# Conditioning by column blocks: shift and scale of the first norm made in four column blocks, with the first pair of row tiles multiplied block by block into held PSUM banks

## The chip, the cores and the metric

The kernel runs on one core of one Trainium2 chip. The metric is the device time of one execution in microseconds; lower is better. The program holds one launch.

## The reference

One layer of a bidirectional encoder is applied to two sequences of 1024 rows and 1024 columns (prompt and sample), each with a conditioning vector c. A final norm follows. Cut to what the change touches:

```python
mod = jax.nn.silu(c) @ w_ada + b_ada
sh1, sc1, ga1, sh2, sc2, ga2 = [m[:, None, :] for m in jnp.split(mod, N_MOD, axis=-1)]
h = rmsnorm(x, g_mix) * (1.0 + sc1) + sh1
z = h @ w_in
q_lat, kv_lat, k_pe, f_in = z[..., :o1], z[..., o1:o2], z[..., o2:o3], z[..., o3:]
y_mla = mla_group(q_lat, kv_lat, k_pe, g_q_lat, w_uq, g_kv_lat, w_ukv)
y_four = fourier_group(f_in, w_four)   # real part of a 2-D FFT, then a small matrix per group
mix = jnp.concatenate([y_mla, y_four], axis=-1) @ w_out
x = x + ga1 * mix
h2 = rmsnorm(x, g_ffn) * (1.0 + sc2) + sh2
ffn = (jax.nn.silu(h2 @ w_gate) * (h2 @ w_up)) @ w_down
return x + ga2 * ffn
```

All is float32. The first two sixths of mod, sh1 and sc1, are the first 2048 columns of w_ada: 8.4 MB that have to be read before any row can be shifted and scaled.

## The kernel before

**Numbers.** A float32 product is made of three matmuls on operands split into a high and a low part (`mm3`, L78 to L80). `split` (L62, L63) makes the parts: a cast on ACT, then a subtraction on DVE that waits for the cast.

**Rows.** The rows of a sequence are reordered so that row tile j and its mirrored tile lie in two tiles u = 0 and 1 of 128 rows. Such a pair k = 0 to 7 (four for each sequence) is the unit of stage 1. For a pair: `x_load` reads the two tiles (0.5 MB each); `norm` squares them on ACT, takes the reciprocal root in six small steps on POOL (`rstd`, L103 to L110) and scales on DVE; `flip` transposes two column groups of 128 at a time on PE and applies scale and shift (s1, sh1) on the way out of PSUM into hf, then splits into hh and hl; `evenodd` adds and subtracts the two halves u on POOL (eo) and splits into eoh and eol; `zproj` multiplies hh and hl by the latent part of the weights (wz, 448 columns, 24 matmuls for each u); `fourier_in` multiplies eoh and eol by the Fourier weights wcs (280 and 256 columns, 24 matmuls each); `latents` transposes the normed latents and stores them.

**Weights.** `prep_wcs` makes a 128-row group of wcs from w_in (loaded as wf) with four matmuls by a small table c2. `wz_split` splits wz. The foldings `fold_q`, `fold_pe` and `fold_out` make products of attention weights and store them for later stages. `extras` is a generator whose pieces lie between the pairs: the rest of `fold_out` and a second pass over w_ada for the gates, 1 MB a chunk.

**Modulation before.** w_ada is read in eight chunks of 128 rows and 2048 columns (`chunk`, 1 MB each). `mod_mm` multiplies each by silu(c), four column groups side by side on 32-wide strips of TensorE, and adds all eight chunks up in one PSUM bank. Only after the eighth can `mod_row` copy the sums out and `mod_vecs` (L146 to L155) transpose them and form s1 and sh1 for all columns; the first `flip` stands behind it.

**Order.** The order on each engine is fixed when the program is built: a scheduler of the framework starts from the order in which the code is written and can move an instruction past others on its engine. At run time each engine takes its list strictly in order and waits on semaphores. Transfers are issued by SP in one list, at most eight in flight; a transfer that waits for an engine holds up all behind it. Tiles with the same tag share memory, so a new tile waits for the last reader of the old one.

**Lines.** w_ada chunk loads L207, their matmuls L216; wf L489, wz L327, x L356; prep_wcs L337 to L347; flip L382 (transposes), L387 and L389 (hf); evenodd L400; zproj's squares L413 and L414, its latents L425 and L426; kv stores L431; latents L440; fold_q L238 and L239; fold_out L251 to L254.

## Time and profile before

| what | value |
|---|---|
| three timed runs | 2041.74, 2043.92, 2044.95 us; median 2043.92 |
| span of the profiled execution (the only time the profile gives for it) | 2043.9 us |
| PE busy in the span | 97% |
| first matmul of the modulation, last chunk's matmul | 11.58 us, 40.80 us |
| s1 and sh1 complete | 45.75 us |
| first product of pair 0 | 48.14 us |
| first product of pair 1 | 81.66 us |
| DMA rate 10 to 20, 20 to 30, 30 to 40 us | 404, 393, 415 GB/s |
| DMA rate 60 to 70 us | 71 GB/s |

The engines are named PE (TensorE matmul), PEld (its weight loads), DVE (VectorE), ACT (ScalarE), POOL (GpSimd) and SP (SyncE, which issues transfers). A row of the timeline has the start, the duration and the operation, the tiles written and read, the shape and the count of instructions merged into it, and in brackets the idle time of the engine just before and what ended it. A float32 matmul that is not split shows as two instructions in the trace, since it takes two passes. The duration of a matmul in a row includes the way through the array; what counts for throughput is the distance from one start to the next.

### The profile page before, as it was taken

Reading aid. Unit: us, or ns where it says so; the run is one execution under the profiler, and the core shown is the slowest. Engines: PE = TensorE matmul, PEld = TensorE weight load, DVE = VectorE, ACT = ScalarE, POOL = GpSimd, SP = SyncE. Lnnn points to the kernel's source line nnn. Section 1 sums busy time; section 2 is a strip of 40 time slices with the busy share of each in tenths; the row PEclk is TensorE's granted clock in tenths of the full one; section 3 lists DMA queues with packets and bytes.
Section 4 is the critical chain, followed back from the end, with each engine's and each line's share of the span. In section 5 each row is a group of like instructions: output and inputs, shape, how many; then the busy total and the mean of one; then the engine's idle time right before and its main releaser. Section 6 shows DMA issues by size and latency. Waiting matters only on the chain.

```text
span 2043.9 us, 27849 instructions
## 1 busy us (share of the span) xinstructions
PE 1986.5 (97%) x9610; PEld 1613.6 (79%) x9610; DVE 1415.6 (69%) x2082; ACT 897.3 (44%) x1741; POOL 832.3 (41%) x1021
## 2 busy tenths in 40 slices
PE   6999999999999999999999999999999999999997
PEld 3788877888787777888888888877788888888876
DVE  3667757766677668878777676777766656667684
ACT  3656635555465554333333365453233333336451
POOL 0555213111313317879779410332654454420142
PEclk8999999999999999999999999999999999999999
DMA  9785694544644375546555587674333232258672
GB/s 363 229 258 180 220 336 132 129 104 106 158 114 129 119 277 192 195 157 210 194 166 196 173 306 251 216 233 140 129 118 103 97 110 103 96 187 276 226 228 89
DMA packets 183817, 370.30 MB, mean 181 GB/s; under 512 B 19004, under 2 KB 60476, under 8 KB 180604
## 3 DMA queue, kind: packets, MB, share of 16 engines
q1 hardware_dynamic: 165004, 310.72, 45.8%
q0 software_dynamic: 18672, 57.81, 9.5%
q8 instruction: 75, 1.23, 0.3%
q14 instruction: 66, 0.54, 0.1%
HBM read 256.46 MB, written 120.39 MB: 184 GB/s over the span
## 4 chain that ended last, share of the span: by engine, by line
PE 52%; DVE 3%; DMA 3%; POOL 1%; issue 1%; ACT 1%; SPq 0%; DVEq 0%; ACTq 0%; POOLq 0%
PE bank L78 17%; PE bank L79 17%; PE bank L80 17%; DVE wl L63 1%; DMA draw<-s_d 1%; ACT wh L62 1%; DMA val<-x_d 1%; DVE val L138 1%; POOL val L138 1%; DMA draw<-t_d 0%; DMA rgu<-in_wgu_dram 0%; DVE val L1610 0%; POOL rs_y L106 0%; DMA draw<-in_w_down_dram 0%; SPq L1570 0%
## 5 line engine op out<-in xcount | busy, mean ns | idle before, releaser
L78 PE MATMUL bank<-H,wh 128*128 128x512 f32 x1224 | 477.8, 390 | 6.9 <-DVE val L138 5.8
L80 PE MATMUL bank<-H,wl 128*128 128x512 f32 x1224 | 476.6, 390 | 0.2 <-DVE wl L63 0.2
L79 PE MATMUL bank<-H,wh 128*128 128x512 f32 x1224 | 476.3, 389 | 0.0
L138 DVE TENSOR_TENSOR val<-bank,val 128x512 f32<-128x512 f32 x244 | 166.7, 688 | 166.9 <-PE bank L80 165.8
L78 PEld LDWEIGHTS bank<-H,wh 128*128 128x128 f32 x1224 | 229.8, 188 | 59.0 <-DVE val L138 8.3
L80 PEld LDWEIGHTS bank<-H,wl 128*128 128x128 f32 x1224 | 229.8, 188 | 50.4 <-DVE wl L63 2.3
L79 PEld LDWEIGHTS bank<-H,wh 128*128 128x128 f32 x1224 | 229.8, 188 | 47.1
L63 DVE TENSOR_TENSOR wl<-draw,wh 128x512 fp32r<-128x512 f32 x286 | 202.2, 740 | 86.3 <-ACT wh L62 85.7
L62 ACT CAST wh<-draw 128x512 fp32r<-128x512 f32 x286 | 169.0, 620 | 158.6 <-PE bank L79 81.6
L79 PE MATMUL bank<-wl,wh 128*128 128x512 f32 x572 | 223.7, 391 | 2.8 <-DVE wl L63 2.8
L138 POOL TENSOR_TENSOR val<-val 128x512 f32<-128x512 f32 x58 | 83.4, 1445 | 343.4 <-DVE val L1584 189.6
L80 PE MATMUL bank<-wh,wl 128*128 128x512 f32 x572 | 222.7, 389 | 0.0
L78 PE MATMUL bank<-wh 128*128 128x512 f32 x572 | 222.6, 389 | 0.0
L62 ACT CAST wh<-rgu 128x512 fp32r<-128x512 f32 x171 | 106.3, 623 | 253.6 <-PE bank L79 192.1
L63 DVE TENSOR_TENSOR wl<-val,wh 128x512 fp32r<-128x512 f32 x133 | 139.7, 1052 | 68.8 <-ACT wh L62 68.7
L63 DVE TENSOR_TENSOR wl<-rgu,wh 128x512 fp32r<-128x512 f32 x171 | 169.1, 989 | 9.7 <-ACT wh L62 9.6
L62 ACT CAST wh<-val 128x512 fp32r<-128x512 f32 x133 | 82.3, 622 | 179.1 <-PE bank L79 156.5
L135 POOL TENSOR_TENSOR val<-rgu 128x512 f32<-128x512 f32 x80 | 114.8, 1435 | 99.2 <-DMA rgu<-in_wgu_dram 95.5
L79 PEld LDWEIGHTS bank<-wl,wh 128*128 128x128 f32 x572 | 107.4, 188 | 28.5 <-DVE wl L63 6.3
L78 PEld LDWEIGHTS bank<-wh 128*128 128x128 f32 x572 | 107.4, 188 | 22.5 <-ACT wh L62 0.2
L80 PEld LDWEIGHTS bank<-wh,wl 128*128 128x128 f32 x572 | 107.4, 188 | 21.9
L135 POOL TENSOR_TENSOR val<-val 128x512 f32<-128x512 f32 x89 | 119.3, 1357 | 1.3
(383 smaller groups left out, 3908.1 us busy)
## 6 DMA issues: line engine op xcount, KB each, us to landing
rgu<-in_wgu_dram SPq DMA_DIRECT2D x86, 512.0 KB
draw<-s_d SPq DMA_DIRECT2D x143, 256.0 KB
s_d<-val POOLq DMA_DIRECT2D x88, 256.0 KB, 3.8
draw<-t_d SPq DMA_DIRECT2D x88, 256.0 KB
s_d<-val SPq DMA_DIRECT2D x66, 256.0 KB
draw<-in_w_down_dram SPq DMA_DIRECT2D x55, 256.0 KB
wada<-in_w_ada_dram SPq DMA_DIRECT2D x13, 1024.0 KB
xt<-in_x_dram SPq DMA_DIRECT2D x16, 512.0 KB
```

The lines of the kernel that those rows point to most:

```text
L62: here["a"] = nc.scalar.copy(hi, src).ins
L63: here["v"] = nc.vector.tensor_tensor(out=lo, in0=src, in1=rd(hi), op=ALU.subtract).ins
L78: nc.tensor.matmul(out, lh, rh, start=first, stop=False, skip_group_check=cont)
L79: nc.tensor.matmul(out, lh, rl, start=False, stop=False, skip_group_check=cont)
L80: nc.tensor.matmul(out, ll, rh, start=False, stop=last, skip_group_check=cont)
L135: return eng.tensor_tensor(out=out, in0=x, in1=y, op=ALU.subtract).ins
L138: return eng.tensor_tensor(out=out, in0=x, in1=y, op=ALU.add).ins
```

## The change

The first 2048 columns of w_ada are laid out anew (wa0) as four blocks. Block b holds, for all 1024 rows, the shift and the scale columns of column groups 2b and 2b + 1. With each block come the raw wf and wz for the same column groups. For each block the kernel multiplies (`block_mm`, 32 matmuls of 128 columns), copies and transposes a short row, forms the two columns of s1 and sh1 for both sequences (`block_vecs`), flips the two groups of pair 0 (`flip(0, b)`), makes their even and odd parts (`evenodd_part`), and adds their part of the four products of pair 0 into four PSUM banks that are held over the loop (`z_mm`, `f_mm`, in `products`, one block late). The evictions become `z_out` and `f_out`. During the loop four banks are left for everything else. fold_q and fold_pe move behind pair 0, with their loads behind the last block; fold_out, the flips of pair 1, the norm of pair 2 and the latents of pair 0 follow in a written order in place of `pair(0)`. The raw wz and two foldings use the tiles of zc and zs of the second sequence, which are made when first needed.

```diff
+        def block_load(b):
+            wt = [w2.tile([P, 4, 512], F32, tag="wada", name="wada", bufs=2) if b % 2 == 0
+                  else w.tile([P, 4, 512], F32, tag=("hh1", "hl1")[i], name="wada1") for i in range(2)]
+            for i in range(2):
+                nc.sync.dma_start(wt[i], a["wa0"][b, i])
+            return wt
+
+        def block_mm(b, wt):
+            pm = bank()[:, :P]
+            for c in range(NC):
+                for j in range(4):
+                    nc.tensor.matmul(pm[32 * j : 32 * j + 32, :], scT[:, c, :], wt[c // 4][:, c % 4, P * j : P * j + P],
+                                     start=(c == 0), stop=(c == NC - 1))
+            mr = stile("modrow")[:, :P]
+            nc.vector.tensor_copy(mr, pm)
+            return mr
...
+        def products(b, u):
+            cs = range(2 * b, 2 * b + 2)
+            z_mm(0, u, pz[u], cs)
+            f_mm(st1["eo", 0][u], u, pc[u], cs)
+
+        for b in range(4):
+            for i in range(2):
+                prep_wcs(2 * b + i, wf[b])
+            wz_split(b, wzr[b])
+            mr = block_mm(b, blk[b])
+            if b > 0:
+                products(b - 1, 0)
+            block_vecs(b, mr)
+            if b > 0:
+                products(b - 1, 1)
+            if b < 2:
+                loads(b + 2)
+            if b == 2:
+                nc.sync.dma_start(ropec, a["ropec"])
+                nc.sync.dma_start(ropes, a["ropes"])
+                x_load(1)
+                fq = fold_loads()
...
+            flip(0, b)
+            evenodd_part(0, b)
+        for u in range(2):
+            z_mm(0, u, pz[u], range(6, 8))
+        norm(1)
+        for u in range(2):
+            z_out(0, u, pz[u])
+        for i in range(2):
+            f_mm(st1["eo", 0, i], i, pc[i], range(6, 8))
+            f_out(0, i, pc[i])
         fold_q(*fq)
-        nc.gpsimd.memset(lw, 0.0)
-        mod_mm(0, 0, ch[0])
-        ch[4] = chunk(4)
...
-        mod_mm(0, 7, ch[7])
-        mod_vecs(mod_row(0), bank, bT, gT, 0, 0, s1, sh1)
-        for g in range(2):
-            flip(0, g)
...
+        fold_pe(wpe, gq)
+        pfirst.close()
+        banks.insert(0, st.enter_context(tc.tile_pool(name="p1_ps", bufs=8, space=PSUM, reuse_waits="tile")))
         nk = len(pairs)
         more = extras()
+
+        x_load(2)
+        next(more)
+        fold_out(0, wo2, wuvT, gq)
+        for g in range(4):
+            flip(1, g)
+        fold_out(1, wo2, wuvT, gq)
+        norm(2)
+        latents(0, 0)
...
-        for k in range(nk - 1):
+        for k in range(1, nk - 1):
             pair(k)
```

How this moves instructions is shown at three places. In the changed file the lines are others: the block matmul is L535, its row's transpose L543, prep_wcs L349, flip L394 with hf at L401, the square of x L378, the squares of the latents L449 and L450, the copies of the Fourier products L505 and L503, x L368, the kv stores L467, the stores of fold_q and fold_pe L254 and L273, the fold_out stores L267, w_out's load L257.

PE before, from the preparation of wcs to the first product; wada and wide are chunks of w_ada in different tiles:

```order
L216 MATMUL bank<-wada,scT 32x512 x4
L337 MATMUL bank<-c_136,wf 128x128 x16
L216 MATMUL bank<-wada,scT 32x512 x4
L216 MATMUL bank<-wide,scT 32x512 x4
L216 MATMUL bank<-wada,scT 32x512 x4
L146 MATMUL bank<-ident,modrow 128x128 x4
L382 MATMUL bank<-ident,xt 128x128 x16
L78 MATMUL bank<-wz_h,hh 128x448
```

PE after, in the loop of blocks, from the preparation of wcs for block 2 to the first half of block 2's matmul (wada, the last row); held is a held bank:

```order
L349 MATMUL bank<-c_130,wf 128x128 x8
L78 MATMUL held<-wz_h,hh 128x448
L79 MATMUL held<-wz_l,hh 128x448
L78 MATMUL held<-wcs_h,eoh 128x280
L79 MATMUL held<-wcs_l,eoh 128x280
L78 MATMUL held<-wz_h,hh 128x448
L79 MATMUL held<-wz_l,hh 128x448
L78 MATMUL held<-wcs_h,eoh 128x256
L80 MATMUL held<-wz_h,hl 128x448
L78 MATMUL held<-wz_h,hh 128x448
L79 MATMUL held<-wz_l,hh 128x448
L535 MATMUL bank<-wada,scT 32x128 x16
```

Before, all flips of pair 0 and all its products stand behind the last chunk's matmul. Now ten products of block 1 stand ahead of the first half of block 2's matmul; thirteen more stand ahead of its second half, and its row's transpose is behind that.

ACT after, from the last block's hf (first row) on; xt in the squares is x of pair 1:

```order
L401 ACTIVATE hf<-bank,sh1b,s1b 128x256
L378 ACTIVATE junk,ms<-xt 128x1024
L62 CAST hh<-hf 128x512
L62 CAST eoh<-eo 128x256 x2
L378 ACTIVATE junk,ms<-xt 128x1024
```

ACT after, a little further, from the Fourier copies of pair 0 to the flips of pair 1; xt in the square is now x of pair 2:

```order
L505 COPY zc_110<-held 128x280
L503 ACTIVATE zs_111<-held,cmask 128x256
L62 CAST kv<-lat 128x128 x2
L378 ACTIVATE junk,ms<-xt 128x1024
L401 ACTIVATE hf<-bank,sh1b,s1b 128x256 x3
L62 CAST hh<-hf 128x512
L401 ACTIVATE hf<-bank,sh1b,s1b 128x256 x2
L62 CAST hh<-hf 128x512
```

ACT before, at the flips of pair 1; the two squares are those of x of pair 2 here too:

```order
L62 CAST kv<-lat 128x128
L413 ACTIVATE junk,mz<-bank 128x256
L414 ACTIVATE junk,mz<-bank 128x128
L366 ACTIVATE junk,ms<-xt 128x1024 x2
L389 ACTIVATE hf<-bank,sh_0_77,s_0_75 128x256
L62 CAST kv<-lat 128x128
L389 ACTIVATE hf<-bank,sh_0_77,s_0_75 128x256 x2
L62 CAST hh<-hf 128x512
```

In both a square of pair 2's x stands ahead of pair 1's hf on ACT. What changed is when that x is asked for. SP before, around the load of pair 2's x (the second row):

```order
L244 DMA wada<-in_w_out_dram 128x2x1024
L356 DMA xt<-in_x_dram 128x1024 x2
L244 DMA wada<-in_w_out_dram 128x2x1024
L260 DMA wq_d<-wq 128x1536
L431 DMA ckv_d_96<-kv 128x128
L431 DMA ckv_d_97<-kv 128x128
```

SP after, around the same load (the sixth row); the two first sequences of kv stores are those of pair 0:

```order
L257 DMA wada<-in_w_out_dram 128x2x1024
L467 DMA ckv_d_94<-kv 128x128
L467 DMA ckv_d_95<-kv 128x128
L467 DMA ckv_d_94<-kv 128x128
L467 DMA ckv_d_95<-kv 128x128
L368 DMA xt<-in_x_dram 128x1024 x2
L254 DMA wq_d<-zraw 256x1x512
L273 DMA wq_d<-wqp 256x1x256
L257 DMA wada<-in_w_out_dram 128x2x1024
```

Before, pair 2's x was asked for ahead of the kv stores of pair 0; now it is asked for behind all four of them.

208 lines of the change are left out of this document (113 added, 95 removed).

## The prediction

> **What bounds the kernel now.** I read the page first, then the busy time by stage, then the order of time on each engine up to 90 us, since only the beginning of the program is rebuilt.
>
> ```profile
> PE 1986.5 (97%) x9610; PEld 1613.6 (79%) x9610; DVE 1415.6 (69%) x2082; ACT 897.3 (44%) x1741; POOL 832.3 (41%) x1021
> PE   6999999999999999999999999999999999999997
> 0.00:20.00 20.00, 10.41 (x48) 4.35 (x48) 2.97 (x10) 1.50 (x2) 1.94 (x9) 1.00 0.83 311
> 20.00:40.00 20.00, 13.55 (x88) 9.76 (x88) 9.62 (x27) 10.10 (x30) 1.74 (x6) 0.82 1.04 404
> 40.00:60.00 20.00, 16.81 (x78) 13.09 (x79) 15.70 (x31) 10.06 (x22) 6.38 (x6) 0.84 0.77 296
> 60.00:81.66 21.66, 17.20 (x88) 12.21 (x86) 14.43 (x29) 12.59 (x30) 13.27 (x31) 0.84 0.56 174
> 81.66:240.00 158.34, 156.15 (x1019) 134.95 (x1018) 108.17 (x237) 94.73 (x242) 75.86 (x168) 1.00 0.69 216
> ```
>
> The columns of a stage are its length, the busy time of PE, PEld, DVE, ACT and POOL (with instructions), the granted clock, the DMA share and GB/s. TensorE (PE) is the bound from 81.66 us on: 156.15 us busy of 158.34. Before that it is busy for 10.41 + 13.55 + 16.81 + 17.20 = 57.97 us of 81.66, so idle for 23.7. From 20 to 40 us the DMA engines are full (404 GB/s), and the modulation weights bound; from 60 to 81.66 they are half idle and a chain through ACT, POOL and DVE bounds. All that the change can win lies in these 23.7 us, and what it wins there arrives at the end of the program, because behind it runs a nearly gapless PE.
>
> ```profile
> 40.80 1.94 PE L216 MATMUL bank<-wada,scT 128*32 128x512 f32 x8 [3.63 <-DMA wada<-in_w_ada_dram]
> 73.25 0.69 PE L78 MATMUL bank<-wcs_h,eoh 128*128 128x280 f32 x1
> 81.66 0.45 PE L78 MATMUL bank<-wz_h,hh 128*128 128x448 f32 x1
> 86.55 1.03 PE L382 MATMUL bank<-ident,xt 128*128 128x128 f32 x8
> ```
>
> The last chunk of w_ada lands at 40.80; the cosine product of the first pair only begins at 73.25; the first product of the second pair runs from 81.66 to 86.55. By 81.66 all of pair 0 and the weight foldings are done, in the changed kernel too, and from there the two kernels' streams hold the same work. So **the gain is 81.66 us less the time at which that product starts after the change**.
>
> **Arrival of the blocks.**
>
> ```profile
> 2.11 0.43 SPq L227 DMA_DIRECT2D wuqT<-in_wuqT_dram  x1
> 5.83 1.62 PE L238 MATMUL bank<-wukT,wuqT 128*128 128x128 f32 x6 [5.83 <-DMA wuqT<-in_wuqT_dram]
> 13.51 0.20 PEld L216 LDWEIGHTS bank<-wada,scT 128*32 128x32 f32 x8 [1.73 <-DMA wada<-in_w_ada_dram]
> ```
>
> By the tile shapes 3.01 MB are in when chunk 1 lands at 13.51, and 13.37 MB when chunk 7 lands at 40.80: 0.38 MB a us. The change asks for 1.05 MB of x and four blocks of 3.08 MB (0.52 of wf, 0.46 of wz, 2.10 of w_ada), 13.37 MB again, with the first large transfer issued behind the small constants at about 3.5 us instead of 1.6. Block 0 is then complete near 17.5 us, a block follows every 8 us, and block 3 is complete between 41 and 42.7, say 41.4: **the loads themselves gain nothing**. A 0.5 MB load takes up to 5.83 - 2.11 = 3.7 us from issue to use.
>
> **The cost of one block.**
>
> ```profile
> 16.00 1.06 PE L216 MATMUL bank<-wide,scT 128*32 128x512 f32 x8 [0.56 <-DMA wide<-in_w_ada_dram]
> 20.07 3.84 PE L337 MATMUL bank<-c,wf 128*128 128x128 f32 x32 [0.44 <-DMA wf<-in_wfT_dram]
> 78.05 0.68 PE L78 MATMUL bank<-wcs_h,eoh 128*128 128x256 f32 x1
> 81.30 0.60 PE L440 MATMUL bank<-ident,lat 128*128 128x128 f32 x4
> ```
>
> The block matmul has 32 matmuls of 32x128, two passes each, 64 in the trace. No row shows that shape. A group of eight 512-wide passes, four column strips abreast, takes 1.06 us, 0.133 each; a quarter of the width gives 0.033, 2.1 us a block and 1.05 for the half behind each transfer. Upwards the bound is a pass of the same width on the full array, 3.84/32 = 0.12, or 7.7 us a block; downwards I exclude a gain, since the same columns stream. I take 0.033, the row of the same line and strips, and keep the other end for a rival. A projection matmul costs 4.89/24 = 0.204 and a Fourier one (81.30 - 78.05)/24 = 0.135, so a block's products (12 of each) are 4.1 us; the preparation of wcs is 16 passes, 1.9 us.
>
> In its third paragraph the section "Wait — 56ns, not 53.3ns?" of the Trainium skill's page "TensorE: Matmul & The Clock Gate" puts a floor of about 25 ns start to start on narrow matmuls, and about 62 ns where matmuls are decoded in software. By 25 ns a block's 64 passes would take 1.6 us, below my 2.1, and nothing changes. By 62 ns they would take 4.0, an estimate that would leave about 2045 us; rival C below is that case, told from rows. The rows here favour the low price: at 16.00 four strips run abreast at 0.133.
>
> ```profile
> 42.80 0.69 DVE L221 COPY modrow<-bank 128x512 f32<-128x512 f32 x1 [1.46 <-PE bank L216]
> 43.64 1.09 PE L146 MATMUL bank<-ident,modrow 128*128 128x128 f32 x4 [0.91 <-DVE modrow L221]
> 45.67 0.56 ACT L389 ACTIVATE hf<-bank,sh,s 128x256 f32<-128x256 f32 x1 [5.61 <-PE bank L382]
> 46.27 0.54 DVE L387 TENSOR_SCALAR hf<-bank,s,sh 128x256 f32<-128x256 f32 x1 [0.52 <-ACT hf L389]
> 47.70 1.30 POOL L400 TENSOR_TENSOR eo<-hf 128x512 f32<-128x512 f32 x1 [19.30 <-DVE hf L387]
> 48.51 1.78 ACT L62 CAST wz_h<-wide 128x896 fp32r<-128x896 f32 x2
> 50.08 2.08 DVE L63 TENSOR_TENSOR wz_l<-wide,wz_h 128x896 fp32r<-128x896 f32 x2
> 50.19 0.62 ACT L62 CAST hh<-hf 128x512 fp32r<-128x512 f32 x1
> 52.08 0.68 DVE L63 TENSOR_TENSOR hl<-hf,hh 128x512 fp32r<-128x512 f32 x1
> 21.67 0.42 DVE L342 TENSOR_TENSOR wcs_l<-bank,wcs_h 128x256 fp32r<-128x256 f32 x1 [9.63 <-ACT wcs_h L341]
> ```
>
> The order shown with the change puts the two halves of block b+1's matmul on PE inside and behind the products of block b, and PE takes them in that order. So the blocks form a loop, whatever has landed. Counted from the end of a block matmul: the row copy (a quarter of 0.69), one transpose and three tiny vector operations end near 1.3 us; hf on ACT (0.56) and then DVE (0.54), one behind the other, end at 2.5. The ACT order has the next block's wz cast (1.78/2 = 0.9) ahead of hh, so hh starts at 2.75 and the first product at 3.4; wz_l (1.04) and hl (0.68) hold DVE until 4.6, or 5.2 where POOL's eo (1.30) runs beside them; eol (two of about 0.42) ends at 5.5 to 6.2. On PE ten products and the first half (1.05) end near 6.8, the rest (2.0) at 8.6, and the second half at 9.2 to 9.8. I take **9.5 us a loop** against 8 us between arrivals: the loop, not DMA, is the new limit. The preparation of the next wcs (1.9) hides in PE's wait between 1.5 and 3.4, its casts behind eol. The four held PSUM banks leave four for all else; in this count each is evicted over 2 us before its next use, so I charge nothing, and where one is not it lengthens the loop by what is missing. So it is with the raw wz and wf in borrowed tiles: their loads wait for splits that end 10 us before the data are due, and 2.1 MB are still in flight then. Block 0's matmul ends at 17.5 + 1.0 = 18.5, block 3's at 18.5 + 3 x 9.5 = **E = 47.0 us**, 5.6 behind its data.
>
> **From E to the second pair.**
>
> ```profile
> 58.37 1.05 ACT L366 ACTIVATE junk<-xt 128x1024 bf16<-128x1024 f32 x1
> 62.32 0.22 POOL L103 TENSOR_SCALAR rs_v<-ms 128x2 f32<-128x2 f32 x1
> 64.54 0.20 POOL L110 TENSOR_TENSOR rs_r<-rs_w,rs_y 128x2 f32<-128x2 f32 x1
> 67.89 0.49 DVE L425 TENSOR_SCALAR lat<-bank,rs_r 128x256 f32<-128x256 f32 x1 [1.38 <-POOL rs_r L110]
> 69.49 0.80 SPq L431 DMA_DIRECT2D ckv_d<-kv  x2
> 72.26 1.49 ACT L389 ACTIVATE hf<-bank,sh,s 128x256 f32<-128x256 f32 x3
> 78.46 0.74 DVE L253 TENSOR_SCALAR so<-bank,gq 128x512 f32<-128x512 f32 x1
> ```
>
> PE is done with pair 0 at about E + 7.5 and then waits. The squares of x (1.05 plus 0.19 of reading out) stand in the order around hh and eoh, the second ends at E + 5.6. POOL then makes three reciprocal roots, 64.74 - 62.32 = 2.4 us each, the last with a slower one: E + 13.0. The latents and the kv split behind it add 1.6. SP issues the load of x 2 only behind the four stores of kv (0.4 each): E + 15.3; it lands 3.7 later, at E + 19.0. ACT's order has the square of x 2 ahead of every hf of pair 1, so **this load is a new wait**: all of pair 1's flips, and DVE's hl and so behind them, stand until it lands. Then ACT needs two squares (2.4), eight hf (1.49/3 = 0.5 each) and four hh (about 0.52), 8.5 us: E + 27.5. The hl of that (0.68) and the eviction (0.74) that frees the product's bank end at E + 28.9 = 75.9. Foldings and flips on PE (8 matmuls in fold_q, 8 of 512 columns, 16 transposes) lie inside these waits; x 1, landing near 45, is covered by the block chain, and the other fold loads by it too. If that cover failed, each would cost its own lateness.
>
> Gain: 81.66 - 75.9 = **5.8 us**. The profile's span is 2043.9 us, the median of the three runs 2043.92, so the same sum holds for both: 2043.9 - 5.8 = 2038.1, **2038 us**. Its own range is 2035 to 2041, from 1 us a loop either way.
>
> **Rivals.**
>
> A. The loop is quicker than the arrivals (its PE and DVE parts overlap better than I stacked them). Then E = 41.4 + 1.0 = 42.4, 4.6 earlier, and the time is **2033.5**. For it: DMA is full in 20 to 40 us. Against: the count of 9.5, in which only about 1 us is generous.
>
> B. It is given back behind E. The second w_ada chunk of the extras is now issued behind the kv stores of pair 1, DVE is by the same count about 5 us behind PE there (xt of x 2, four evictions and four eol stand ahead of the latents), and PE comes out of a wait:
>
> ```profile
> 66.00:70.00 4.00, 4.00 (x12) 2.35 (x11) 2.21 (x8) 1.28 (x4) 3.35 (x11) 0.50 0.02 6
> ```
>
> After such a wait the clock was 0.50 from 66 to 70. A first product at that clock for 3.4 us costs 1.7, a late chunk 2 to 3: about 4 us lost, **2042**, no change that a measurement can tell.
> The section "Part 1: The HAM clock gate (the "warmup" mystery)" of the same page of the Trainium skill says that one idle window of about 3.4 us halves the clock; the row at 66 agrees, and by that rule the new wait would cost an estimated 1.7 us.
>
> C. The narrow strips do not run four abreast at a quarter of the price. At 0.12 a pass the half block costs 3.8, the loop 5.6 more, E 3 x 5.6 + 2.8 = 19.6 more: **2057.7**, slower. It decides from 0.033 + 5.8/224 = 0.059 us a pass (224 passes lie on the path); at 0.062 the time is near 2045. Against it: the strips in the row at 16.00, and no sign of an issue limit there.
>
> That the order does not do what the edit says is excluded by the order itself.
>
> **How the numbers follow.** Forecast 0.50, A 0.20, B 0.20, C 0.10. A measurement of this kernel can tell about 0.2%, 4.1 us. Faster takes A and 0.42 of the forecast's 0.50; same takes the remaining 0.08 and 0.18 of B; slower takes C and 0.02 of B: 0.62, 0.26, 0.12. For the range I leave out the dear end of C and the far end of A: 2032 to 2046.
>
> **What would show it.** The order in time at the start: block matmuls of L535 ending about 9.5 us apart, the last near 47 (A: 8 apart, 42.4; C: 12 or more apart, single passes far above 0.033). ACT's square of x idle before it on the load of x near 62 to 66. The product of pair 1 (L78, bank from hh) starting near 76. From there PE gapless; a gap on w_ada in pair 1, or a clock of 0.50 under its first product, is B. I would be wrong altogether if the PE gaps after that start were not those of before.

## The result and the profile after

The changed kernel takes 2054.07 us, the median of five runs from 2052.87 to 2055.22, against 2043.74 of the kernel before in runs beside it (2039.7 to 2044.95). The ratio is 1.0052, with a 95% interval of 1.0039 to 1.0065: **slower by half a per cent**, where 2038 us was forecast, with a range to 2046. The profiled execution spans 2053.4 us, 9.5 more than before.

The page of the changed kernel (first line) and its busy time by stage, in the same columns as before, cut at the start of pair 1's first product:

```profile
PE 1992.6 (97%) x9802; PEld 1620.0 (79%) x9802; DVE 1407.9 (69%) x2092; ACT 898.7 (44%) x1745; POOL 833.1 (41%) x1025
...
0.00:20.00 20.00, 8.63 (x84) 7.23 (x85) 5.24 (x16) 6.39 (x13) 3.67 (x15) 1.00 0.81 301
20.00:40.00 20.00, 18.86 (x215) 15.81 (x213) 11.84 (x27) 8.66 (x22) 4.54 (x4) 1.00 1.02 405
40.00:60.00 20.00, 16.24 (x159) 12.97 (x147) 11.00 (x30) 10.53 (x29) 6.90 (x12) 1.00 0.48 179
60.00:81.56 21.56, 14.16 (x48) 8.57 (x48) 9.95 (x28) 10.04 (x22) 8.02 (x19) 0.76 0.58 194
81.56:110.00 28.44, 25.12 (x141) 18.93 (x140) 18.74 (x37) 13.59 (x34) 12.69 (x31) 0.94 0.85 266
```

From 20 to 40 us PE is now nearly full (18.86 of 20, before 13.55): the block loop does what it says. From 60 to 81.56 PE is emptier than before, and the granted clock is 0.76. New is the last row: PE was gapless from pair 1 on before, and now it is idle for 3.3 us and throttled before 110 us.

The order of time on VectorE and TensorE at the landmarks of the prediction: the copies of block 0's and block 3's row, pair 1's first product, and the second latents of pair 3 (L476), by which both kernels have done the same work; the last row is that of the kernel before:

```profile
18.82 0.29 DVE L538 COPY modrow<-bank 128x128 f32<-128x128 f32 x1 [1.76 <-PE bank L535]
50.82 0.29 DVE L538 COPY modrow<-bank 128x128 f32<-128x128 f32 x1 [2.60 <-PE bank L535]
81.56 0.60 PE L78 MATMUL bank<-wz_h,hh 128*128 128x448 f32 x1
152.31 0.60 PE L476 MATMUL bank<-ident,lat 128*128 128x128 f32 x4
...
142.62 0.60 PE L440 MATMUL bank<-ident,lat 128*128 128x128 f32 x4
```

The last block's matmul ends at 50.75, just ahead of its copy, not at 47.0. Pair 1 starts at 81.56 and not at 75.9: 0.1 us earlier than before (81.66). So the expected gain was gone before pair 1. And the same latents start at 142.62 in the kernel before: 9.7 us later now, lost **between** pair 1's start and pair 3, where the prediction expected nothing. What follows is alike: 1901.1 us from these latents to the end of the span, 1901.3 before.

TensorE's rows on the chunks of the gate row (L228), which the extras multiply during pairs 1 to 3; the last row is chunk 1 in the kernel before:

```profile
87.65 1.58 PE L228 MATMUL bank<-wada,scT 128*32 128x512 f32 x8
100.82 1.82 PE L228 MATMUL bank<-wada,scT 128*32 128x512 f32 x4 [3.32 <-DMA wada<-in_w_ada_dram]
104.03 1.21 PE L228 MATMUL bank<-wada,scT 128*32 128x512 f32 x4
109.42 1.05 PE L228 MATMUL bank<-wada,scT 128*32 128x512 f32 x4
111.41 1.05 PE L228 MATMUL bank<-wada,scT 128*32 128x512 f32 x4
124.93 1.05 PE L228 MATMUL bank<-wada,scT 128*32 128x512 f32 x4
126.23 1.05 PE L228 MATMUL bank<-wada,scT 128*32 128x512 f32 x4 [0.24 <-DMA wada<-in_w_ada_dram]
...
94.86 1.06 PE L216 MATMUL bank<-wada,scT 128*32 128x512 f32 x8
```

Before, every chunk was one group of eight (two passes of four strips) in 1.06 or 1.07 us, without a wait. Now PE waits 3.32 us for chunk 1, and chunks 1 and 2 stand at two places each in PE's order, one for each of the two 512 KB transfers of a chunk; chunk 4 waits between its halves. A half uses two strips of the four and takes 1.05 us, as much as the whole. The granted clock behind the wait:

```profile
100.80:105.20 4.40, 4.38 (x14) 1.57 (x14) 0.69 (x1) 1.94 (x5) 2.39 (x7) 0.61 1.06 306
```

4.40 us at 0.61 cost some 1.7. Why chunk 1 is late stands on SP's queue, first of the changed kernel, then of the kernel before:

```profile
88.83 2.02 SPq L267 DMA_DIRECT2D wo_d<-so  x2
90.90 0.92 SPq L368 DMA_DIRECT2D xt<-in_x_dram  x2
94.80 1.86 SPq L467 DMA_DIRECT2D ckv_d<-kv  x2
96.75 0.86 SPq L219 DMA_DIRECT2D wada<-in_w_ada_dram  x2
```

```profile
86.10 1.49 SPq L207 DMA_DIRECT2D wada<-in_w_ada_dram  x2
90.83 0.80 SPq L431 DMA_DIRECT2D ckv_d<-kv  x2
```

Before, chunk 1 was issued at 86.10, ahead of pair 1's kv stores. Now it is issued at 96.75, behind them and behind the last stores of the out foldings and the load of x 3. SP waits on the way for the evictions of the out foldings on VectorE (so), and for the splits of the latents (kv), which follow their scaling on VectorE.

### The profile page after: what moved, and what is told of

It is laid out like the page before. It is cut to its first block, busy times and chain, and to the rows that moved or that the text cites. A ratio compares the mean times of both kernels' runs of the same rounds, so it can differ in the third digit from the quotient of the medians.

```text
span 2053.4 us, 28277 instructions
## 1 busy us (share of the span) xinstructions
PE 1992.6 (97%) x9802; PEld 1620.0 (79%) x9802; DVE 1407.9 (69%) x2092; ACT 898.7 (44%) x1745; POOL 833.1 (41%) x1025
## 4 chain that ended last, share of the span: by engine, by line
PE 53%; DVE 3%; DMA 2%; issue 1%; POOL 1%; SPq 0%; ACT 0%; DVEq 0%; ACTq 0%; POOLq 0%
PE bank L79 18%; PE bank L78 18%; PE bank L80 18%; DVE wl L63 1%; DMA draw<-t_d 1%; DVE val L139 1%; DMA val<-x_d 1%; POOL val L139 1%; DMA draw<-s_d 0%; ACT wh L62 0%; DVE val L1692 0%; SPq L1651 0%; DVE val L1585 0%; SPq L1652 0%; POOL rs_v L105 0%
## 5 line engine op out<-in xcount | busy, mean ns | idle before, releaser
L79 PEld LDWEIGHTS bank<-wl,wh 128*128 128x128 f32 x572 | 107.3, 188 | 29.3 <-DVE wl L63 7.1
```

The costliest lines, as they stand in the source:

```text
L79: nc.tensor.matmul(out, lh, rl, start=False, stop=False, skip_group_check=cont)
```

## The experiments

Two questions: what takes the 9.7 us behind pair 1's start, and why pair 1 doesn't start earlier. Theory T1 for the first is the chunks (late, split, and the slow clock behind a wait), T2 that VectorE and the loop are behind and the chunks only show it. The names T1, T1a, T3, L1 and so on are those of the expectations. The landmarks of all runs, from their profiles (us; "copy" is the copy of the last block's row), with the times of the timed runs:

| kernel | copy | first product of pair 1 | its distance from the copy | second latents of pair 3 | median | ratio to before, interval |
|---|---|---|---|---|---|---|
| before | | 81.66 | | 142.62 | 2043.7 | |
| changed | 50.82 | 81.56 | 30.7 | 152.31 | 2054.1 | 1.0052 [1.0039, 1.0065] |
| one chunk only | 50.21 | 81.57 | 31.4 | 143.41 | 2044.9 | 0.9998 [0.9987, 1.0010] |
| one DMA a chunk | 50.42 | 83.61 | 33.2 | 147.27 | 2050.8 | 1.0037 [1.0023, 1.0050] |
| chunk 1 early | 49.10 | 80.65 | 31.6 | 150.25 | 2052.2 | 1.0043 [1.0022, 1.0064] |
| chunks on ACT's queue | 50.82 | 83.69 | 32.9 | 151.83 | 2053.6 | 1.0043 [1.0028, 1.0057] |
| wz split late (every engine's order as in changed) | 49.25 | 82.47 | 33.2 | 149.69 | 2054.8 | 1.0053 [1.0038, 1.0068] |
| x 2 early | 50.82 | 80.69 | 29.9 | 149.08 | 2050.5 | 1.0033 [1.0020, 1.0046] |
| fold_q first | 50.52 | 79.31 | 28.8 | 147.43 | 2049.3 | 1.0031 [1.0021, 1.0040] |
| fold_q late | 49.73 | 80.25 | 30.5 | 148.24 | 2051.1 | 1.0033 [1.0021, 1.0046] |
| three edits | 50.75 | 80.02 | 29.3 | 144.98 | 2046.6 | 1.0017 [1.0007, 1.0027] |
| three edits, fold_q late | 49.33 | 77.71 | 28.4 | 141.35 | 2044.5 | 1.0007 [0.9998, 1.0017] |
| the same, other banks | 50.60 | 79.01 | 28.4 | 142.31 | 2043.6 | 1.0000 [0.9990, 1.0010] |
| foldings first | 49.22 | 76.53 | 27.3 | 138.19 | 2043.7 | 0.9991 [0.9981, 1.0002] |
| foldings first, other banks, fold_pe | 50.44 | 77.01 | 26.6 | 139.66 | 2043.9 | 0.9997 [0.9986, 1.0008] |
| foldings first, other banks | 50.74 | 76.50 | 25.8 | 140.47 | 2042.3 | 0.9994 [0.9985, 1.0002] |
| before, one DMA a chunk | | 81.62 | | 142.58 | 2044.3 | 1.0004 [0.9994, 1.0014] |

The last row is a second look at the head of the kernel before: it repeats to 0.04 us, while the rest of its span is 1905.9 us instead of 1901.3. Single runs of one kernel lie some 3 us around its median. The changed kernel's head repeats less well. The row "wz split late" is the same program as the changed kernel, instruction by instruction (shown below), so these two rows are two executions of one program: they differ by 1.6 us at the copy, by 2.5 from there to pair 1, and by 3.5 from pair 1 to the latents. A difference of that size between two profiles does not show an effect of an edit by itself. The start of pair 1's flips repeats better: 21.1 to 21.4 us behind the copy in the six runs whose order is the same up to there.

### One chunk only

```diff
-                    nxt = mod_load(c + 1, cols1, wada_tile())
+                    nxt = wt
```

> Edit: the extras load chunk 0 of w_ada alone and multiply it eight times (the gate row is then computed from one chunk; 7 MB of loads are left out), so that no matmul of pairs 1 to 3 waits for a chunk and none is split. T1 (of the 9.6 us lost between 88 and 130 us, the chunks' waits, the half clock behind them and the split matmuls are all but about 1): pairs 1 and 2 run without a wait of PE, the lag to the kernel before at the latents of pair 3 is 0.5 to 2 us instead of 9.7, 2044 to 2046.5. Rival T2 (VectorE's backlog holds pairs 1 and 2 and the chunks only show it): waits for latents or evictions take their place, 2048 or more.

Two latents and the stages behind pair 1's start in this run:

```profile
99.56 0.60 PE L476 MATMUL bank<-ident,lat 128*128 128x128 f32 x4
143.41 0.60 PE L476 MATMUL bank<-ident,lat 128*128 128x128 f32 x4
...
81.57:110.00 28.43, 28.43 (x182) 23.48 (x184) 20.31 (x40) 13.67 (x34) 14.81 (x31) 1.00 0.87 274
```

PE is busy for 28.43 of 28.43 us. This is the run that decides. It starts pair 1 within 0.01 us of the changed kernel, so that the two can be laid side by side. At the two latents of pair 1 the changed kernel lags it by 94.33 - 93.93 = 0.4 and 106.05 - 99.56 = 6.5 us, at those of pair 2 by 7.6 and 8.9, and at 143.41 still by 8.9. These steps are chunk 0 (1.58 instead of 1.07), chunk 1 (6.1: the wait of 3.32, a second group of 1.0, and the slow clock, 1.7), chunk 2 (1.15, its second group) and chunk 4 (1.3, its second group and a wait of 0.24). T1 holds: 8.9 of the 9.8 us that pairs 1 to 3 take longer are the chunks (5.4 of 6.3 by the second execution of the changed kernel), and VectorE's backlog by itself is worth at most the remaining 0.9. What it does by holding up SP, and so chunk 1, is part of the chunks' share. The run also leaves out 7 MB of loads. That these cost nothing by themselves is shown by the run with the foldings first (below): it loads all eight chunks, waits for none, and takes 61.7 us from pair 1's start to the latents, where this run takes 61.8 and the kernel before 61.0. Over all runs, that stretch took 67.2 to 70.8 us with two DMAs a chunk (seven runs) and 61.7 to 65.0 with one (seven runs).

### One DMA a chunk, chunk 1 early, chunks on another queue

```diff
-            for j, (lo_, n) in enumerate(cols):
-                nj = n // 512
-                nc.sync.dma_start(
-                    wt[:, j * nj : (j + 1) * nj, :],
-                    a["w_ada"][c * P : (c + 1) * P, lo_ : lo_ + n].rearrange("p (j n) -> p j n", n=512))
+            nc.sync.dma_start(
+                wt.rearrange("p (g j) n -> p g (j n)", g=2),
+                a["w_ada"][c * P : (c + 1) * P, :].rearrange("p (g d) -> p g d", g=2)[:, :, 2 * D : 3 * D])
```

> Edit: each w_ada chunk of the extras comes by one DMA for both column groups instead of two of 512 KB, so that the order of the changed kernel no longer puts the two halves of the matmuls of chunks 1 and 2 at two places (a half alone took 1.05 us on two strips, all four strips 1.06 us). Theory T1 (what is lost lies in pairs 1 and 2: a load of chunk 1 issued late, a 3.32 us wait of PE for it, the half clock behind it and the split chunk matmuls, 9.6 us in all between 88 and 130 us): the two split chunks go, 2 us, the wait for chunk 1 stays or grows as the whole chunk has to land; time 2051 to 2053 (changed kernel: 2054.1), latents of pair 1 second half start 104 to 106 us (106.05 in the changed kernel, 99.06 before). Theory T2 (the loss is in the loop of blocks and the chain behind it, and pairs 1 and 2 only show waits that move): no change, within 1 us.

```profile
78.56 3.46 PE L262 MATMUL bank<-wada,wuvT 128*128 128x512 f32 x4 [2.94 <-ACT junk L376]
102.09 1.07 PE L226 MATMUL bank<-wada,scT 128*32 128x512 f32 x8 [1.57 <-DMA wada<-in_w_ada_dram]
```

The gain is larger than expected and partly given back. From pair 1's start to the latents this run takes 147.27 - 83.61 = 63.7 us, against 70.7 in the changed kernel and 61.8 with one chunk only: the whole chunk stands later in PE's order and its wait shrinks to 1.57 at full clock. But pair 1 starts 2 us later here: PE waits 2.94 us at 78.56, where the changed kernel waits 0.88, and the clock behind it is slow (0.79 from 76 to 84). PE's order up to there is that of the changed kernel, and 33.2 us behind the copy is what the second execution of that kernel has too, so nothing ties this to the edit.

```diff
             fold_out(3, wo2, wuvT, gq)
+            nxt = mod_load(1, cols1, wada_tile())
             yield
...
-                if c + 1 < NC:
+                if 0 < c and c + 1 < NC:
```

> Edit: the load of chunk 1 of the extras is issued one step earlier, right behind the stores of the last out folding and ahead of the loads of x3 and of pair 1's kv stores on SP's queue; nothing else moves. T1: SP issues it at about 90 us instead of 96.75, it lands at 94 to 95; PE's wait of 3.32 us, the half clock behind it (about 1.6 us) and the split of chunk 1's matmuls (1 us) go; time 2047 to 2049.5; the lag to the kernel before at the second latents of pair 1 is 1 to 2 us instead of 7.0. T2: PE waits instead for chunk 2 or for the latents; less than 2 us of the 10 come back, 2052 or more.

```profile
94.62 1.05 PE L228 MATMUL bank<-wada,scT 128*32 128x512 f32 x4 [0.25 <-DMA wada<-in_w_ada_dram]
105.69 1.79 PE L228 MATMUL bank<-wada,scT 128*32 128x512 f32 x4 [2.17 <-DMA wada<-in_w_ada_dram]
```

T1's lag came (100.08 at the second latents of pair 1, 1.0 behind the kernel before), but not its time; 2052.2 is T2's. Chunk 1's wait goes (0.25 and 0.22 are left), and chunk 2 takes its place with 2.17 us, a half and a slow clock of its own, because its load still stands behind kv stores. The whole row of loads is late, not one of them. That T2's reason is nevertheless wrong is shown by the run with one chunk only.

```diff
-                nc.sync.dma_start(
+                nc.scalar.dma_start(
                     wt[:, j * nj : (j + 1) * nj, :],
```

> Edit: the chunk loads of the extras are issued on ScalarE's queue instead of SP's; nothing else of the changed kernel is altered. Theory T1a (the chunks are late because their issue stands on SP behind the foldings' stores, x3 and pair 1's kv stores, all of which wait for VectorE): chunk 1 issues at 84 to 88 instead of 96.75, chunk 2 some 6 us later; the wait of 3.32 us and the half clock go and no chunk waits over 1 us; 2047 to 2050. Rival T1b (the chunks are late because the two slots come free late, or because the 16 DMA engines are full): PE still waits 2 us or more for chunk 1 or 2, 2051.5 or more.

```profile
84.32 4.32 ACTq L219 DMA_DIRECT2D wada<-in_w_ada_dram  x2
...
97.70 0.63 PE L476 MATMUL bank<-ident,lat 128*128 128x128 f32 x4 [1.60 <-DVE lat L461]
```

The first half of T1a holds: on ScalarE's queue chunk 1 is issued at 84.32, and PE waits for none of chunks 1 to 3. So SP's order made it late, not the slots. The time did not follow, and 2053.6 lies in the rival's range: PE waits 1.60 us for the latents, and chunks 4, 5 and 7 are split or late. As a remedy the run settles nothing.

### The path from the last block to pair 1

Rows of the changed kernel, on SP, DVE, ACT and PE, behind the last block's matmul at 50.75:

```profile
62.59 4.34 SPq L467 DMA_DIRECT2D ckv_d<-kv  x4
65.41 0.60 DVE L251 SCALAR_TENSOR_TENSOR zraw<-bank,gq,gkvr 128x128 f32<-128x128 f32 x2
65.81 1.22 PE L250 MATMUL bank<-wukT,zraw 128*128 128x128 f32 x4 [6.31 <-DVE zraw L251]
67.02 0.86 SPq L368 DMA_DIRECT2D xt<-in_x_dram  x2
70.78 1.06 ACT L378 ACTIVATE junk<-xt 128x1024 bf16<-128x1024 f32 x1 [4.95 <-DMA xt<-in_x_dram]
72.16 2.65 PE L394 MATMUL bank<-ident,xt 128*128 128x128 f32 x16
73.26 1.48 ACT L401 ACTIVATE hf<-bank,sh1b,s1b 128x256 f32<-128x256 f32 x3 [1.33 <-PE bank L394]
79.47 0.65 ACT L62 CAST hh<-hf 128x512 fp32r<-128x512 f32 x1
```

There are two paths. On one, x 2 is loaded behind four kv stores and ACT waits 4.95 us for it, as predicted. On the other, fold_q's evictions (zraw) stand on VectorE behind the z outputs, at 65.41; PE waits 6.31 us for them, and has the flips of pair 1 behind fold_q, at 72.16. Behind that wait PE also ran at a granted clock of 0.50 (64.15 to 68.15) and 0.54 (to 74.15): the four 512-wide folding matmuls at 68.75 took 3.62 us, those at 74.65 1.88. The second path ended last: x 2's first square is done at 71.93, and ACT then waits 1.33 us more for the flips.

```diff
         for u in range(2):
             z_mm(0, u, pz[u], range(6, 8))
+        x_load(2)
         norm(1)
...
-        x_load(2)
         next(more)
```

> Edit: the loads of x2 are issued behind the last block's z products in program order, ahead of the four kv stores of pair 0 that held them on SP's queue until 67.02 us. The prediction's new wait (ACT waits 4.95 us for x2 at 70.78, with all of pair 1's evictions behind it): that wait goes, evictions of pair 1's flips start at 69 to 70 instead of 72.7, the first product of pair 1 at 77.5 to 79.5 instead of 81.56. T1: what follows keeps its shape, shifted, the wait for chunk 1 stays (its load stands behind kv stores that come as much earlier): 2050.5 to 2052. T2: the whole gain of 2 to 4 us reaches the end and nothing more. Rival: PE waits for the fold_out stores or DVE instead, pair 1 starts where it did, 2054.

```profile
73.25 1.48 ACT L401 ACTIVATE hf<-bank,sh1b,s1b 128x256 f32<-128x256 f32 x3 [5.20 <-PE bank L394]
```

The wait for x 2 is gone, and it was not the one that counted: ACT now waits 5.20 us for the flips instead, which start at 72.15 as they did, and the first hf stands at 73.25 as it did. Pair 1 starts 0.87 us earlier, not the 2 to 4 of T1. The time, 2050.5, is at the low end of T1's all the same; chunk 1 was issued at 93.36 here, and PE's wait for it was 0.70.

```diff
         for u in range(2):
             z_mm(0, u, pz[u], range(6, 8))
+        for i in range(2):
+            f_mm(st1["eo", 0, i], i, pc[i], range(6, 8))
+        fold_q(*fq)
         norm(1)
...
-            f_mm(st1["eo", 0, i], i, pc[i], range(6, 8))
             f_out(0, i, pc[i])
-        fold_q(*fq)
```

> Edit: the folding into the query weights (its eight matmuls and their evictions) stands ahead of pair 1's norm and of the two z outputs instead of behind them. Theory T1 for the time from the last block's matmul to pair 1: PE waits 6.31 us (to 65.81) because the folding's evictions stand on VectorE behind the z outputs' scalings, which wait for three rstd's in a row on GpSimd, and the flips of pair 1 stand on PE behind the folding. So the folding ends 3 to 5 us earlier, flips of pair 1 start at 67 to 69 (72.16), first product at 77 to 79 (81.56), 2050 to 2052 (changed kernel 2054.1). Rival T3 (the path runs over x2's load, ScalarE and PE's own work): first product at 80.5 or later, 2053 or more.

With this edit the order also brings x 2's load forward, ahead of the kv stores. Flips at 67.45, first product at 79.31, 28.8 us behind the copy instead of 30.7. T1's flips came; the first product is 0.3 us past its range, and the time (2049.3) is below it. Two things moved at once, so the share of each is open.

```diff
-        fold_q(*fq)
-        fold_pe(wpe, gq)
...
-        fold_out(0, wo2, wuvT, gq)
         for g in range(4):
             flip(1, g)
+        fold_q(*fq)
+        fold_pe(wpe, gq)
+        fold_out(0, wo2, wuvT, gq)
         fold_out(1, wo2, wuvT, gq)
```

> Edit: the folding into the query weights stands behind the flips of pair 1 instead of ahead of them; x2's load stays behind pair 0's kv stores. T1: flips start as soon as the scaled x1 is there (59.7 in the changed kernel), at 60 to 61 instead of 72.16, evictions on ScalarE at 61 to 67; then PE's 11 us of foldings, latents; first product of pair 1 at 75 to 78, 2048 to 2051. T3: first product at 80.5 or later.

The first rows of the flips in this run:

```profile
61.29 2.81 PE L394 MATMUL bank<-ident,xt 128*128 128x128 f32 x16 [3.76 <-DVE lat L462]
75.02 2.95 PE L264 MATMUL bank<-wada,wuvT 128*128 128x512 f32 x4 [3.62 <-DMA wada<-in_w_out_dram]
```

The flips start 11 us earlier (9.8 counted from the copy), and pair 1 no earlier (30.5 us behind the copy): the foldings and latents that PE has ahead of it now wait for the second rows of w_out, loaded behind x 2 on SP (3.62 us). T1's 75 to 78 did not come; 80.25 is just short of T3's 80.5. And there is a wait that no step of the prediction has: the flips wait 3.76 us for the scaling of the latents, which they don't read.

The next edit was to ask for the loop of blocks, the other part of the way to pair 1.

```diff
-            wz_split(b, wzr[b])
             mr = block_mm(b, blk[b])
...
             evenodd_part(0, b)
+            wz_split(b, wzr[b])
```

> Edit: the split of wz's block b stands behind the evictions of block b instead of ahead of its matmul, so that its ScalarE cast (0.93 us) and VectorE difference (1.48 us) leave the chain from a block's matmul to the next one. Theory L1 (the loop of 10.45 us a block is the chain over VectorE, ScalarE and GpSimd): 9.3 to 9.9 us a block, the last block's matmul ends at 47.5 to 49.5 instead of 50.75, pair 1 starts as much earlier, 2051.5 to 2053. Rival L2 (GpSimd's sums and differences at 2.27 us and PE's products set the loop, or the split now holds the products that need it): the end stays at 50 or later, 2054 or more.

On ACT in this run:

```profile
29.95 0.93 ACT L62 CAST wz_h<-zraw 128x896 fp32r<-128x896 f32 x1
30.78 0.61 ACT L62 CAST hh<-hf 128x512 fp32r<-128x512 f32 x1
```

The edit did not reach the program. In the built order the split stands where it stood: the cast of wz is still ahead of hh, and on every engine all instructions follow in the order of the changed kernel, from the first to the last. So neither L1 nor L2 was tested. What the run gives is a second execution of the changed kernel. Its copies of the four rows are at 17.80, 28.32, 38.73 and 49.25, 10.5, 10.4 and 10.5 us apart, where the first execution has 11.1, 10.4 and 10.5; its median, 2054.8, is within 0.8 us of the first.

What the loop is made of is read from rows of the changed kernel, first POOL and DVE, then PE, between the copies at 29.88 and 40.31:

```profile
32.27 2.27 POOL L426 TENSOR_TENSOR eo<-hf 128x256 f32<-128x256 f32 x2 [8.18 <-DVE hf L399]
33.88 1.22 DVE L63 TENSOR_TENSOR hl<-hf,hh 128x512 fp32r<-128x512 f32 x1
...
33.02 0.47 PE L78 MATMUL held<-wz_h,hh 128*128 128x448 f32 x1 [0.24 <-ACT hh L62]
35.03 0.39 PE L78 MATMUL held<-wcs_h,eoh 128*128 128x256 f32 x1 [0.61 <-ACT eoh L62]
35.96 1.08 PE L535 MATMUL bank<-wada,scT 128*32 128x128 f32 x32
39.17 1.08 PE L535 MATMUL bank<-wada,scT 128*32 128x128 f32 x32
```

The halves of the block matmul (1.08 for 32 passes, 0.034 a pass) cost what was forecast. PE waits 0.24 and 0.61 us and is busy in its order otherwise: from 33.02 to 39.17, less the first half of 1.0, the products take 5.1 us with the wait, where I counted 4.1. The 0.61 goes back to POOL: ACT's cast of eoh at 34.58 had itself waited 1.13 us for the second half of eo. That a shorter eo would shorten the loop was not tried.

### Together

> Edit: the three edits above together (one DMA a chunk, chunk 1 issued early, x2 issued early). T1: the gains add up, 2 plus 5 plus 2 to 4 us: 2043 to 2046, at or a little below the kernel before (2043.7); first product of pair 1 at 77.5 to 79.5. T2: 2048 or more.

The three edits (one DMA a chunk, chunk 1 early, x 2 early) gave 2046.6, 0.6 past T1's range and under T2's; pair 1, at 80.02, missed T1's 77.5 to 79.5. PE still waits 1.18 and 1.57 us for chunks 0 and 1.

> Edit: the folding into the query weights behind the flips of pair 1, x2's load ahead of the kv stores, one DMA a chunk of the extras and chunk 1 issued early (all of these edits; the three last alone gave 2046.6 with pair 1 starting at 80.02). T1: pair 1 starts at 74 to 77; the chunk loads of the extras, which stand behind the stores of the foldings on SP's queue, come as much earlier; 2041 to 2044, at or below the kernel before (2043.5). Rival: the chunk loads don't come earlier, as the DMAs or SP's queue hold them, PE waits for them, 2045 to 2047.

The latents of pair 3 start 1.3 us earlier than in the kernel before, with 2044.5 in time: the loss is undone, no more. T1's numbers were missed by 0.7 us at pair 1 and by 0.5 in time, and the rival's time did not come either; PE waits 1.01 and 1.13 us for chunks 3 and 5.

```diff
         for i in range(2):
             f_mm(st1["eo", 0, i], i, pc[i], range(6, 8))
+        x_load(2)
+        next(more)
+        fold_q(*fq)
+        fold_out(0, wo2, wuvT, gq)
+        fold_out(1, wo2, wuvT, gq)
         norm(1)
         for u in range(2):
             z_out(0, u, pz[u])
...
```

Not shown are the places where the same calls stood, the edits of the chunks' loads as above, and a rule that puts fold_q's evictions ahead of the scaling of x 1 on VectorE.

> Edit: one DMA a chunk and chunk 1 issued early (as before), x2 and the second pair of w_out rows loaded right behind the last block, and the folding into the query weights and the first two out foldings ahead of pair 1's norm and of the z outputs, their evictions on VectorE ahead of the scaling of x1. Theory: from the last block's matmul to pair 1 the engines stand idle behind three rstd's on GpSimd; foldings that fill this time are off the path: PE's waits between 54 and 66 us shrink from some 8 us to 3 or less, flips of pair 1 at 61 to 64, pair 1's first product at 72 to 75 (81.56 in the changed kernel, 77.7 with the query folding behind the flips), no wait over 1 us for chunks: 2037 to 2041, below the kernel before (2043.2). Rival: the z outputs, now later, hold the latents and PE's order with them, or the chunks are late again: pair 1 at 77 or later, 2043 or more.

```profile
68.06 3.65 PE L395 MATMUL bank<-ident,xt 128*128 128x128 f32 x16 [3.36 <-DVE lat L463]
```

No wait of PE for a chunk shows in this run, and the latents of pair 3 start 4.4 us earlier than before. Flips (68.06) and pair 1 (76.53) come later than expected, held again by the latents' scaling, and the time, 2043.7, is the rival's. The medians don't show the 4.4: 0.9991, with an interval that includes no change.

The cause of that wait was tested by one edit: the held banks are taken in the order f, z, z, f instead of z, z, f, f. The first flip of pair 1 gets the first of them, and z is read by that scaling.

```diff
-        pz = [held_bank(u) for u in range(2)]
-        pc = [held_bank(2 + i) for i in range(2)]
+        pc = [held_bank(2)]
+        pz = [held_bank(u) for u in range(2)]
+        pc.append(held_bank(3))
```

> Edit: the run with the foldings ahead of pair 1's norm (flips at 68.06 after a wait of 3.36 us, 18.8 us behind the copy of the last block's row; pair 1's first product 27.3 us behind it), with the held banks taken in the other order and nothing else; every engine's order is the same. Theory B (held z banks): flips 14 to 16 us behind that copy, first product 24 to 26 us behind it, 1 to 3 us less than there; 2040 to 2043. Rival V (VectorE's queue): flips 18 us or more behind, first product within 0.5 us of 27.3.

```profile
65.96 1.47 PE L395 MATMUL bank<-ident,xt 128*128 128x128 f32 x12
68.74 0.66 PE L395 MATMUL bank<-ident,xt 128*128 128x128 f32 x4 [1.31 <-DVE so L264]
70.87 0.63 PE L477 MATMUL bank<-ident,lat 128*128 128x128 f32 x4 [1.47 <-DVE lat L463]
```

With every engine's order the same, the flips start 15.2 us behind the copy instead of 18.8, and the wait in front of them is gone: it was the bank. The next waits, for the evictions of the foldings and for the latents themselves, take most of it back; pair 1 starts 1.5 us earlier, counted from the copy, which is within what two executions of one program differ by. And PE waits 1.94 us for chunk 2, which the run without this edit did not.

> Edit: as the run with the query folding behind the flips, x2 early, one DMA a chunk and chunk 1 early (2044.5; flips at 60.88 and again waiting at 64.15 for the scaling of the latents, pair 1's first product at 77.71), and the held banks taken in the other order; nothing else. Theory B: flips at 59 to 60 with no wait for the latents' scaling, but the foldings behind them still wait for VectorE, so that pair 1 starts 0 to 2 us earlier, 76 to 77.7; 2042.5 to 2044.5. Rival V: as before, within 0.5 us in the profile.

On the base with the query folding behind the flips, the same edit: the flips start at 59.26 without that wait, and pair 1 is no earlier (28.4 us behind the copy, as without the edit): the same scaling now holds PE behind the flips, for 2.59 us at fold_q's matmuls at 65.45.

```diff
         fold_q(*fq)
+        fold_pe(wpe, gq)
         fold_out(0, wo2, wuvT, gq)
...
-        fold_pe(wpe, gq)
         pfirst.close()
```

> Edit: as the run with the foldings ahead of pair 1's norm (profiled span 2038.3, pair 1's first product at 76.53), and the four held PSUM banks are taken in another order, so that the bank which the first flip of pair 1 gets is that of the f product, read early, and not that of z; the pe folding stands directly behind the query folding. Theory B (the held z banks hold the flips: 68.06 with a wait of 3.36 us for the scaling of the latents): flips start at 64.5 to 65.5, directly behind the two out foldings, pair 1's first product at 72.5 to 74.5; 2039 to 2042 against 2043.5 of before, faster than before by 0.1 to 0.2%. Rival V (VectorE's queue and not the bank): flips at 67 or later, first product at 76 or later, no change against 2043.7.

With fold_pe moved as well as the banks: flips at 64.36, directly behind the out foldings, as the theory said, then 2.39 us for the evictions of the out foldings. Pair 1 at 77.01 and the time are the rival's; the gain expected did not come.

> Edit: the kernel before, each chunk of the extras by one DMA for both column groups; nothing else. Theory R (the edit repairs what the change brought: split matmuls and late chunks): no change, ratio 0.999 to 1.001, pair 1's first product at 81 to 83 and the second latents of pair 3 at 142 to 144. Rival G (the edit helps any version of this stage): faster by 0.1% or more.

In that kernel the same helper loads the chunks of shift and scale, which then come from the columns of the gates; amounts and shapes are the same. There is no change within 0.14%: the edit repairs what the change brought.

## Why the prediction was wrong

- **"From there the two kernels' streams hold the same work", so "the gain is 81.66 us less the time at which that product starts".** This is the step that failed: the work is the same, its loads are not where they were. Pairs 1 to 3 took 9.8 us longer, 8.9 of them for the chunks (one chunk only). Rival B had the mechanism: the second chunk, which is chunk 1, issued behind pair 1's kv stores, and a slow clock. It priced them at about 4 us, with a chance of 0.20. It expected the slow clock under pair 1's first product, where the granted clock was 1.00 (81.56 to 97); it came behind the wait for the chunk. What it lacked is the rest of the 8.9: I did not see that chunks 1 and 2 stand in two halves in PE's order, although the order of the changed kernel has them so, nor that chunk 4 would fall into two.
- **Arrival and the strips.** Block 0's matmul ended at 18.76 (18.5), in part by luck: its second half began with its load at 16.82 and took 1.94 us, not 1.05. In the later blocks a half cost 1.08 us, as forecast. Rival C is out.
- **"9.5 us a loop".** Mis-sized: 11.1, 10.4 and 10.5, so that E was 50.75 and not 47.0. The start of the first product (3.2 us behind the block's matmul, 3.4 forecast) was right; the products took 5.1 and not 4.1, with 0.61 of it waiting for eoh, and POOL and VectorE beside one another were slower than their rows alone. Rival A is out with it. This alone would have made 2041.9 of 2038.1, past the forecast's own range of 1 us a loop (2041) and inside the outer one.
- **"E + 28.9".** Mis-sized by 1.9: the third root ended at E + 12.9 (13.0), x 2 was issued at E + 16.3 (15.3), ACT's last hh ended at E + 29.4 (27.5 for all). The new wait on x 2 was there, 4.95 us, but it was not what ended last. "Foldings and flips on PE (...) lie inside these waits" failed: fold_q waits behind the z outputs on VectorE and the flips behind fold_q, at a half-speed clock, and this second path ended 1.33 us after the first; without the wait for x 2 only 0.87 us came.
- **The sum** closes for the profiled execution: the 5.8 us less 3.75 and 1.9 leave 0.1 of gain, and 9.8 of loss make 2043.9 - 0.1 + 9.8 = 2053.6 against a span of 2053.4. In the second execution of the same program pair 1 starts 0.8 us later than before and pairs 1 to 3 take 6.3 longer, with a span of 2050.0. How much of the loss falls before pair 1 changes from one execution to the next; most of it falls behind it in both.
- **The sign of the change itself.** With its loads mended and the foldings moved, the block scheme shortens the head by 2 to 4 us in three profiles (latents of pair 3 at 138.19 to 140.47 against 142.6), the direction of the forecast, though two executions of one program differ by 2.6 there. Whether the kernel before would gain as much from moved foldings was not run. In time no version is shown to be faster than the kernel before: 0.9991 and 0.9994, with upper ends of 1.0002.

## What to carry to other kernels

A rebuilt beginning ends only where the next stage's loads are back in step: compare not just when that stage starts, but what stands ahead of its loads on the issuing queue. A tile filled by two transfers may be used at two places, and a matmul on half the strips costs as much as on all of them. When a wait is taken away, look for the path that ends just behind it; here x 2 early uncovered the flips, fold_q late the rows of w_out, the foldings first a held bank, and the other banks the evictions. And look at the order of the built program before reading a run: one edit of the source here changed nothing in it.

## What the runs showed of the hardware

The slow clock did not need a long wait, and the same wait did not always bring it. PE waits 2.2 us for hh behind the last block in all fifteen runs with blocks, ending between 52 and 54 us. In eight of them the granted clock fell to half behind it, in seven it stayed full. First the run with x 2 early, then the run with the three edits:

```profile
54.00:58.00 4.00, 3.86 (x21) 3.34 (x22) 1.92 (x5) 3.38 (x14) 2.09 (x6) 1.00 0.60 227
```

```profile
54.00:58.00 4.00, 3.92 (x11) 3.49 (x12) 1.92 (x5) 2.26 (x8) 2.08 (x6) 0.50 0.61 228
```

Behind the 2.17 us for chunk 2 in the run with chunk 1 early it was 0.54 over 3.6 us. By the traces' records of the clock, all slow stretches that begin in the first 170 us of these runs last 3.41, 6.83 or 10.24 us, steps of 3.41. Laid on a grid of 3.41 us through its own slow stretches, each of the eight runs has 1.54 to 2.22 us of this wait in one step, and each of the seven at most 1.44. So where the wait falls on the grid decided. The line at about 1.5 us holds for this wait alone: a wait of 1.57 us for chunk 1 in the run with the three edits lay in one step (94.36 to 97.77), and the clock stayed at 1.00.

The section "Part 1: The HAM clock gate (the "warmup" mystery)" of the Trainium skill's page "TensorE: Matmul & The Clock Gate" says that the clock halves after an idle window of about 3.4 us, and that the window runs freely. The free window and its length agree with these rows. That the window has to be idle as a whole does not, since 1.54 us of idle time in it were enough, and the measurement decides.

POOL's two halves of eo took 2.27 us at 32.27 beside a busy VectorE, and 1.41 at 53.21 in the last block, where VectorE stood idle for 1.0 us beside it. VectorE's hl took 1.22 us at 33.88, beside POOL's eo, and 0.69 at 75.28 in pair 1.
